# Outputs and last gates of a hybrid encoder layer, made in pairs of pieces

## The chip, the cores and the metric

The kernel runs on one core of one Trainium2 chip. The metric is the device time of one execution in microseconds (us); every time given for the kernel before is the median of three runs, 1471.24 us (1471.11 to 1471.32). Traces are taken from one profiled execution of the same program. The engines are called PE (TensorE, matmuls), PEld (TensorE's weight loads), DVE (VectorE), ACT (ScalarE), POOL (GpSimd) and SP (SyncE); SP, POOL and ACT also issue DMAs.

## The reference, cut to what matters

One encoder layer for T = 1088 frames (1024 of a new stream, 64 of a running one), model width 1024, in fp32. All parts but the norms are matrix products:

```python
proj = xn @ w_in                                   # 1024 -> 5120
cb, cc, ch, q, k, v, ga, gb = split(proj)
cv, conv_state = causal_conv(cc * ch, conv_prefix, w_conv)
ya = (cb * cv) @ w_conv_out                        # 512 -> 1024, "u" is cb * cv
o, new_k, new_v = attn_fn(heads(q), heads(k), heads(v))   # 8 heads of 64
yb = o.reshape(B, L, ATT_DIM) @ w_attn_out         # 512 -> 1024
merged = sigmoid(ga) * ya + sigmoid(gb) * yb
x = x + merged @ w_out                             # 1024 -> 1024
x = x + (silu(xn2 @ w1) * (xn2 @ w3)) @ w2         # d_ff = 2816
```

The change concerns the gates `ga` and `gb`, the two output products `ya` and `yb`, and the start of the products with `w1` and `w3` (the "up" units).

## The kernel before, in words

**Numbers as pairs.** Every fp32 operand is held as a high part, rounded to the fast format by ACT, and a low part, the rest, formed by DVE (`split`, lines 128 and 129). A product is then three matmuls: weight high with x high, weight high with x low, weight low with x high.

**Stages, in order of time.** Norm and transposition of x, and the projection of v; projections for q, k, cc, ch, cb and six of the eight row blocks of gb as seven-product (Strassen-like) units (`run`, line 269); gates ga (eight blocks of 128 rows) and the last two blocks of gb as plain products (`gate`, `product`, lines 333 to 335), with the attention threaded between them; outputs ya and yb with the merge (lines 1097 to 1124); the product with `w_out` (`wo`, lines 1163 to 1168) with the second norm; the up units a0, b0, a1, b1, ... (`run` again); the down products (line 1682).

**Pieces.** T = 1088 columns are four pieces of 272 (`PIECES`; HN = 272, HT = 544). `product` makes one piece: for each block k of 128 rows the three matmuls, all into one PSUM bank. A gate has 8 blocks k, so 24 matmuls a piece; an output block (`ya`, `yb`) has 4, so 12 matmuls a piece. `run` on the other hand works on two pieces, j = 0 and 1, in two banks of one tile [128, 2, 512], and goes (high, high) j = 0, j = 1, then (high, low) j = 0, j = 1, then (low, high) j = 0, j = 1: each weight stands for two matmuls in a row.

**Gates and attention.** The first four gates begin with their pieces 0 and 1, since the right half of x is being loaded again. Then come their pieces 2 and 3 and gates 4 to 7, piece by piece; after each piece `between` emits 3.15 steps of the attention (scores, softmax, transposition, values; 72 of them and three to drain). The last two gates (LAST = 2) stand behind the attention. Gate pieces use three banks (`pmm`); the attention uses five (`patt`, two buffers of two banks, and `ppv`, one). ACT copies a piece to SBUF (line 815, `st_pool`, five buffers) and POOL's queue stores it to DRAM.

**Order of instructions.** The tile framework orders the instructions of every engine at build time: in the program's order, except that an instruction which its own estimate of times finds not ready yet is passed by later ones that are. Engines then run their queue strictly in that order. `tc.issue_after(x)` keeps the instructions of a block behind `x` where they are on the same engine as `x`. A new pool on the place of a closed one waits for the closed pool's tiles.

**Outputs.** When the attention is done, `u` and `ob` (the attention's output) are loaded and split into two tiles; then for two row blocks at a time come ya, ya, yb, yb. Each piece has a bank of `psum2` (five buffers). On a ya piece DVE multiplies by the sigmoid (line 1108); on a yb piece DVE multiplies (1119), adds (1120), and the sum is split into `mg`, the operand of the later products, and, for the 64 frames of the running stream, into `ms`. `gates_in` loads the rows of ga and gb again, ga in four DMAs of a piece each.

**Up units.** Unit a0 (`r0`) and unit b0 (`r1`) are emitted by hand around the last transpositions. The seven steps of a unit are the products 1, 2, 6, 7, 5, 4, 3. a0's and b0's steps 1 and 2 come first, then a0's 6, 7, 5, 4, 3 (behind b0's step 2), then b0's 6 (its third step), 7, 5, 4, 3. `shot` copies (line 257, ACT) keep a product that a later step adds to in the same bank: the snapshot "7" must be taken before step 4 writes.

Of the kernel before, what the change touches and what calls it, by code (L numbers as in the profile page):

```python
# [20 lines left out]
T = TP + TS  # L21
# [11 lines left out]
HT = T // 2  # L33
HN = HT // 2
# [3 lines left out]
LAST = 2  # L38
# [17 lines left out]
class Acts:  # L56
# [3 lines left out]
        self.t = t  # L60

    def at(self, l, k, o, n):
        return self.t[:, l, k, o : o + n]


@with_exitstack
def encoder_kernel(ctx: ExitStack, tc: tile.TileContext, ins, outs):
    nc = tc.nc
    mm = nc.tensor.matmul
    vec, act, pool_e = nc.vector, nc.scalar, nc.gpsimd  # L70
# [24 lines left out]
    u_d = dr.tile([4, P, T], F32, name="u_d")  # L95
# [30 lines left out]
    def split(hi, lo, src):  # L126

        a = act.copy(hi, src)  # L128
        b = vec.tensor_tensor(lo, src, hi.bitcast(F32), op=ALU.subtract)  # L129
        return a.ins, b.ins  # L130
# [11 lines left out]
    taken = [-1]  # L142
# [183 lines left out]
    def product(out, w, x, o, n):  # L326

        kt = 4 * len(w)
        for k in range(kt):
            a, b = (t[:, k % 4] for t in w[k // 4])  # L330
            p, q = x.at(0, k, o, n), x.at(1, k, o, n)
            first, then = (q, p) if x is xn and o // HN % 2 == 0 else (p, q)
            mm(out, a, first, start=k == 0, stop=False)  # L333
            mm(out, a, then, start=False, stop=False)  # L334
            mm(out, b, p, start=False, stop=k == kt - 1)  # L335
# [471 lines left out]
    def gate(i, cs):  # L807
        g, m = GATES[i]
        dst = ga_d if g == "a" else gb_d
        for c in cs:  # L810
            o, n = PIECES[c]
            ps = pmm.tile([P, 512], F32, tag="mm", name=f"g{i}_{c}")
            product(ps[:, :n], gate_w[i], xn, o, n)
            st = st_pool.tile([P, HN], F32, tag="st", name=f"gst{i}_{c}")
            act.copy(st[:, :n], ps[:, :n])
            nc.gpsimd.dma_start(dst[m * P : (m + 1) * P, o : o + n], st[:, :n])

    gate_w = {}
# [216 lines left out]
    sg = {}  # L1035

    def gates_in(nm, m):
        t = row_tile(int(nm == "ga"), f"{nm}{m}")
        if nm == "gb":
            nc.sync.dma_start(t, gb_d[m * P : (m + 1) * P])  # L1040
        for o, n in PIECES:
            sg[nm, m, o] = t[:, o : o + n]
            if nm == "ga":
                nc.sync.dma_start(t[:, o : o + n], ga_d[m * P : (m + 1) * P, o : o + n])

    head_load(0)

# [11 lines left out]
    for i in range(4, len(GATES)):  # L1059
        gate_w[i] = next_w()  # L1060
        if i == len(GATES) - LAST:
            for _ in steps:
                pass
            att_stack.close()
            uo = pg_stack.enter_context(tc.tile_pool(name="uo", bufs=1, reuse_waits="tile"))
            both_x = []
            for nm, pad in (("u", 56), ("ob", 48)):
                uo.tile([P, pad], F32, name=f"pad_{nm}")
                t = uo.tile([P, 2, 4 * T + 8], F32R, name=nm)[:, :, : 4 * T]
                both_x.append(Acts(t.rearrange("p l (k t) -> p l k t", k=4)))  # L1070
            u, ob = both_x
            for q in range(4):
                u_ld = nc.sync.dma_start(u.t[:, 1, q].bitcast(F32), u_d[q])
                u_cast = split(u.t[:, 0, q], u.t[:, 1, q], u.t[:, 1, q].bitcast(F32))[0]
            for k in range(2):
                split(ob.t[:, 0, k], ob.t[:, 1, k], o_rows[k])
            late_r = row_tile(1, "rc2"), row_tile(0, "rc3")
            gates_in("ga", 0)
            gates_in("gb", 0)
            for k, r in zip((2, 3), late_r):  # L1080
                o = ob.t[:, 0, k].bitcast(F32)
                with tc.issue_after(u_ld.ins):
                    nc.sync.dma_start(o, o_d[k * P : (k + 1) * P])
                    ld = rc_load(r, k)
                vec.tensor_tensor(r, o, r, op=ALU.mult)
                split(ob.t[:, 0, k], ob.t[:, 1, k], r)
            with tc.issue_after(ld):
                gates_in("ga", 1)
        for c in range(4):
            gate(i, (c,))  # L1090
            between()


    mg = quarters("mg")
    ms = mspool.tile([P, KD, 2, TS], F32R, tag="ms", name="ms")
    psum2 = pg_stack.enter_context(tc.tile_pool(name="psum2", bufs=5, space=PSUM, reuse_waits="tile"))
    for m0 in range(0, 8, 2):
        for m in (m0, m0 + 1):
            wa = next_w()
            if m0:  # L1100
                gates_in("ga", m)
            for o, n in PIECES:
# [5 lines left out]
                vec.tensor_tensor(t, ya[:, :n], t, op=ALU.mult)  # L1108
        for m in (m0, m0 + 1):
            wb = next_w()  # L1110
            if m:
                gates_in("gb", m)
            for o, n in PIECES:
# [3 lines left out]
                yb = psum2.tile([P, 512], F32, tag="mm", name=f"yb{m}_{o}")  # L1117
                product(yb[:, :n], wb, ob, o, n)
                vec.tensor_tensor(z, yb[:, :n], z, op=ALU.mult)
                vec.tensor_tensor(t, t, z, op=ALU.add)  # L1120
                split(mg.at(0, m, o, n), mg.at(1, m, o, n), t)
                h, a = o // HT, 512 - o % HT
                if a < n:
                    split(ms[:, m, 0, 32 * h : 32 * h + 32], ms[:, m, 1, 32 * h : 32 * h + 32], t[:, a:])
    pg_stack.close()


# [62 lines left out]
    if True:  # L1190
# [578 lines left out]
```

## Time and profile before

| what | value |
|---|---|
| median of three runs | 1471.24 us |
| the profiled execution | 1472.42 us, of which the span of the trace is 1470.3 us |
| matmuls, and weight loads | 10176 each |
| gates, first two pieces of gates 0 to 3 | 344.4 to 368.4 us |
| attention and gate pieces | to 552.1 us |
| rest of the last two gates | 552.1 to 572.9 us |
| outputs ya and yb | 572.9 to 668.9 us |
| product with w_out, second norm | 668.9 to 770.7 us |
| up units | 770.7 to about 1230 us |

A row of a timeline has the start in us from the span's start, the duration, the engine, the source line, the operation, the output and the inputs by the program's names, the shapes, and in brackets how long the engine was idle before and what released it. A row by windows has the stretch, its length, and for each engine the busy time and, in brackets, the count of instructions that touch the stretch. A row by tile has the count, the shortest, median and longest duration in ns, and the first and last start. Matmul durations overlap: what counts for PE is the distance between starts.

### The profile page before, as it was taken

What the parts mean: (1) busy time and instruction counts of PE and PEld (TensorE: products, weight loads), DVE (VectorE), ACT (ScalarE), POOL (GpSimd) and SP (SyncE); (2) the same over time, 40 slices, a digit from 0 to 9 for tenths busy, and PEclk for the clock granted to TensorE, in tenths of its full rate; (3) what the DMA queues carried; (4) which work ended last, traced back from release to release, by engine and by line L of the source; (5) the groups of instructions that cost most, each with busy time, mean ns of one, the idle gap of its engine ahead of it and who ended that gap; (6) DMA issues with size and microseconds to landing.
All of it is one profiled execution on the core that took longest, in us unless ns stands there. A gap on an engine that the chain in (4) does not pass through costs nothing.

```text
span 1470.3 us, 26411 instructions
## 1 busy us (share of the span) xinstructions
PE 1455.5 (99%) x10176; PEld 1366.9 (93%) x10176; DVE 983.1 (67%) x1856; ACT 679.7 (46%) x1391; POOL 136.5 (9%) x249
## 2 busy tenths in 40 slices
PE   8999999999999999999999999999999999999997
PEld 6899999999989899998889999999999999888886
DVE  7975565641677775753588767666666768957677
ACT  7654333332777776531355444444444445512223
POOL 1400010001111111000100111110011111000000
PEclk9999999999999999999999999999999999999999
DMA  8687522237776657434432443443344448867686
GB/s 280 185 274 227 182 78 94 66 111 228 209 192 180 182 172 244 158 126 136 154 108 80 153 168 139 168 150 123 122 153 168 147 168 305 286 228 245 219 265 208
DMA packets 163133, 260.26 MB, mean 177 GB/s; under 512 B 18784, under 2 KB 98848, under 8 KB 163008
## 3 DMA queue, kind: packets, MB, share of 16 engines
q1 hardware_dynamic: 142080, 192.79, 41.6%
q0 software_dynamic: 19776, 63.70, 12.1%
q10 hardware_dynamic: 1152, 2.10, 0.4%
q8 instruction: 80, 1.31, 0.4%
q14 instruction: 45, 0.37, 0.1%
HBM read 170.67 MB, written 89.70 MB: 177 GB/s over the span
## 4 chain that ended last, share of the span: by engine, by line
PE 92%; DVE 3%; DMA 3%; ACT 1%; issue 1%; SPq 1%; ACTq 0%; DVEq 0%
PE Ab L269 9%; PE Aa L269 8%; PE A L1682 8%; PE Db L269 4%; PE Da L269 4%; PE D L1682 4%; PE Agb L269 2%; PE Bb L269 2%; PE Ba L269 2%; PE B L1682 2%; PE wo L1163 2%; PE wo L1165 2%; PE wo L1164 2%; PE g L335 2%; PE g L334 2%; PE g L333 2%
## 5 line engine op out<-in xcount | busy, mean ns | idle before, releaser
L333 PE MATMUL g<-xn,wp 128*128 128x272 f32 x320 | 93.7, 293 | 0.0
L335 PE MATMUL g<-xn,low 128*128 128x272 f32 x320 | 93.4, 292 | 0.0
L334 PE MATMUL g<-xn,wp 128*128 128x272 f32 x320 | 92.7, 290 | 0.0
L128 ACT CAST ring<-w2r 128x512 fp32r<-128x512 f32 (+1 forms) x78 | 43.2, 588 | 98.4 <-PE A L1682 50.7
L865 DVE CUSTOM_DVE_ANT_0 p<-s,bb 128x640 f32<-128x640 f32 (+5 forms) x72 | 47.5, 660 | 38.5 <-DMA qd<-q_d 26.2
L1682 PE MATMUL A<-ring,low 128*128 128x512 f32 x264 | 72.3, 389 | 0.0
L1682 PE MATMUL A<-ring,ht 128*128 128x512 f32 x264 | 72.3, 390 | 0.0
L129 DVE TENSOR_TENSOR low<-rawa,wa 128x512 fp32r<-128x512 f32 x55 | 37.7, 687 | 41.7 <-ACT wa L128 41.7
L335 PEld LDWEIGHTS g<-xn,low 128*128 128x128 f32 x320 | 60.3, 188 | 0.5
L333 PEld LDWEIGHTS g<-xn,wp 128*128 128x128 f32 x320 | 60.3, 188 | 0.5
L334 PEld LDWEIGHTS g<-xn,wp 128*128 128x128 f32 x320 | 60.2, 188 | 0.5
L1682 PEld LDWEIGHTS A<-ring,ht 128*128 128x128 f32 x264 | 49.4, 188 | 10.6 <-ACT acc L1692 0.4
L1682 PEld LDWEIGHTS A<-ring,low 128*128 128x128 f32 x264 | 49.6, 188 | 10.3
L269 PE MATMUL Ab<-tt,wb 128*128 128x272 f32 x352 | 57.8, 285 | 1.3 <-ACT wb L128 1.3
L129 DVE TENSOR_TENSOR ring<-w2r,ring 128x512 fp32r<-128x512 f32 (+1 forms) x78 | 49.0, 646 | 13.4 <-ACT ring L128 13.2
L269 PE MATMUL Ab<-mg,wb 128*128 128x272 f32 x352 | 58.0, 285 | 0.0
L269 PE MATMUL Aa<-tt,wa 128*128 128x272 f32 x352 | 57.8, 285 | 0.0
L269 PE MATMUL Aa<-mg,wa 128*128 128x272 f32 x352 | 57.7, 285 | 0.0
L875 ACT ACTIVATE p<-p,mx 128x640 f32<-128x640 f32 (+5 forms) x72 | 50.8, 706 | 11.4 <-DVE mx L865 10.1
L128 ACT CAST wa<-rawa 128x512 fp32r<-128x512 f32 x55 | 34.0, 621 | 47.4 <-PE Ab L269 33.3
L128 ACT CAST wb<-rawb 128x512 fp32r<-128x512 f32 x55 | 34.0, 620 | 38.7 <-PE Aa L269 24.5
L1163 PE MATMUL wo<-low,mg 128*128 128x512 f32 x128 | 50.9, 397 | 0.0
(554 smaller groups left out, 4547.9 us busy)
## 6 DMA issues: line engine op xcount, KB each, us to landing
h_d<-hq POOLq DMA_DIRECT2D x44, 512.0 KB, 4.4
ht<-h_d SPq DMA_DIRECT2D x77, 256.0 KB, 3.9
low<-h_d SPq DMA_DIRECT2D x77, 256.0 KB, 3.7
h_d<-hq_early POOLq DMA_DIRECT2D x29, 512.0 KB, 4.6
rawa<-in_w_ff SPq DMA_DIRECT2D x11, 1024.0 KB, 6.2
rawb<-in_w_ff SPq DMA_DIRECT2D x11, 1024.0 KB, 5.5
w2r<-in_w_ff SPq DMA_DIRECT2D x11, 1024.0 KB, 7.9
qd<-q_d SPq DMA_DIRECT2D x32, 272.0 KB, 4.1
```

Source lines behind the costliest of these rows:

```text
L128: a = act.copy(hi, src)
L129: b = vec.tensor_tensor(lo, src, hi.bitcast(F32), op=ALU.subtract)
L269: newest[0] = mm(t[:, j, :HN], w[:, k, :], x[p][:, k, l, j * HN : (j + 1) * HN], start=p in (1, 2, 7) and k == 0 and n == 0, stop=k == 3 a ...
L333: mm(out, a, first, start=k == 0, stop=False)
L334: mm(out, a, then, start=False, stop=False)
L335: mm(out, b, p, start=False, stop=k == kt - 1)
L865: vec.tensor_tensor_reduce(out=s if len(ps.shape) == 2 else s.rearrange("p (a b) -> p a b", a=2), in0=ps, in1=bias if len(ps.shape) == 2 e ...
L875: act.activation(s, s, AF.Exp, bias=mx, scale=-1.0, accum_out=sm)
L1163: mm(ps, x(k, 0), wh, start=f, stop=False)
L1164: mm(ps, x(k, 1), wh, start=False, stop=False)
L1165: mm(ps, x(k, 0), wl, start=False, stop=e)
L1682: mm(t, ht[k][:, j, x], w[:, l], start=p in (1, 2, 7) and k == 0 and n == 0, stop=k == len(ks) - 1 and n == 2, skip_group_check=p in (6, 5 ...
```

## The change

Gate pieces that are emitted two at a time are now made in the order of `run` by the new `product2`: the first pieces of gates 0 to 3, in two of the three `pmm` banks, and both halves of the last two gates, in a two-bank tile. The outputs are made in halves of 544 columns, also with `product2`; DVE and ACT work on a half at once, and ga's rows come in two DMAs instead of four. `psum2` is opened when the attention's pools close, with two buffers of two banks instead of five of one; the last two gates use it too. `st_pool` has three buffers instead of five. `u` and `ob` get a layout in which each half of 544 has 32 more words behind it and the low parts lie 40 words further; the low parts of their weights start at the slot's beginning instead of 40 words on, and the skipped slot before `w_out` is no longer skipped. In the up stage, b0's third step is put behind the last matmul of a0.

```diff
 class Acts:
     def at(self, l, k, o, n):
-        return self.t[:, l, k, o : o + n]
+        h = o // HT
+        a = h * (HT + 32) + o - h * HT
+        return self.t[:, l, k, a : a + n]
...
+    def product2(outs, w, x, o):
+
+        kt = 4 * len(w)
+        for k in range(kt):
+            a, b = (t[:, k % 4] for t in w[k // 4])
+            for n, (s, l) in enumerate(((a, 0), (a, 1), (b, 0))):
+                for j in range(2):
+                    mm(
+                        outs[j], s, x.at(l, k, o + j * HN, HN),
+                        start=k == 0 and n == 0, stop=k == kt - 1 and n == 2,
+                    )
...
-            {"src": ins[nm][0][:, m * P : (m + 2) * P], "w": 2 * P, "at": 40}
+            {"src": ins[nm][0][:, m * P : (m + 2) * P], "w": 2 * P}
...
-    st_pool = pg_stack.enter_context(tc.tile_pool(name="st_pool", bufs=5, reuse_waits="tile"))
+    st_pool = pg_stack.enter_context(tc.tile_pool(name="st_pool", bufs=3, reuse_waits="tile"))
...
     def gate(i, cs):
         g, m = GATES[i]
         dst = ga_d if g == "a" else gb_d
-        for c in cs:
+        if i >= len(GATES) - LAST:
+            two = psum2.tile([P, 2, 512], F32, tag="mm", name=f"g{i}_{cs[0]}")
+            pss = [two[:, j] for j in range(2)]
+        else:
+            pss = [pmm.tile([P, 512], F32, tag="mm", name=f"g{i}_{c}") for c in cs]
+        if len(cs) == 2:
+            product2([ps[:, :HN] for ps in pss], gate_w[i], xn, PIECES[cs[0]][0])
+        else:
+            product(pss[0][:, :HN], gate_w[i], xn, *PIECES[cs[0]])
+        for c, ps in zip(cs, pss):
             o, n = PIECES[c]
-            ps = pmm.tile([P, 512], F32, tag="mm", name=f"g{i}_{c}")
-            product(ps[:, :n], gate_w[i], xn, o, n)
             st = st_pool.tile([P, HN], F32, tag="st", name=f"gst{i}_{c}")
             act.copy(st[:, :n], ps[:, :n])
...
             att_stack.close()
+            psum2 = pg_stack.enter_context(tc.tile_pool(name="psum2", bufs=2, space=PSUM, reuse_waits="tile"))
...
-        for c in range(4):
-            gate(i, (c,))
-            between()
+        if i < len(GATES) - LAST:
+            for c in range(4):
+                gate(i, (c,))
+                between()
+        else:
+            gate(i, (0, 1))
+            gate(i, (2, 3))
...
-    psum2 = pg_stack.enter_context(tc.tile_pool(name="psum2", bufs=5, space=PSUM, reuse_waits="tile"))
...
-            for o, n in PIECES:
+            for o in HALVES:
                 t = sg["ga", m, o]
                 with tc.issue_after(u_cast):
                     act.activation(t, t, AF.Sigmoid)
-                ya = psum2.tile([P, 512], F32, tag="mm", name=f"ya{m}_{o}")
-                product(ya[:, :n], wa, u, o, n)
-                vec.tensor_tensor(t, ya[:, :n], t, op=ALU.mult)
+                ya = psum2.tile([P, 2, 512], F32, tag="mm", name=f"ya{m}_{o}")
+                product2([ya[:, j, :HN] for j in range(2)], wa, u, o)
+                t = t.rearrange("p (j n) -> p j n", j=2)
+                vec.tensor_tensor(t, ya[:, :, :HN], t, op=ALU.mult)
...
         two_sums = early.tile([P, 2, D], F32, tag="raw", name="two_sums")
-        taken[0] += 1
         w = wo_half(0)
...
             r = up_run(n, this, ahead)
+        if n == 1:
+            with tc.issue_after(newest[0]):
+                next(r)
         for _ in r:
```

The loop of yb is changed in the same way, with the add and both splits on halves.

More of the change, by code (lines that the diff above doesn't have):

```diff
@@ L62, in at, with rows @@
     def at(self, l, k, o, n):
-        return self.t[:, l, k, o : o + n]
+        h = o // HT
+        a = h * (HT + 32) + o - h * HT
+        return self.t[:, l, k, a : a + n]
+    def rows(self, l, k):
+        return self.t[:, l, k].rearrange("p (h t) -> p h t", h=2)[:, :, :HT]
 @with_exitstack
@@ L1035, in encoder_kernel @@
     sg = {}
+    HALVES = (0, HT)
     def gates_in(nm, m):
@@ L1064, in encoder_kernel @@
             att_stack.close()
+            psum2 = pg_stack.enter_context(tc.tile_pool(name="psum2", bufs=2, space=PSUM, reuse_waits="tile"))
             uo = pg_stack.enter_context(tc.tile_pool(name="uo", bufs=1, reuse_waits="tile"))
             both_x = []
[L1067 removed]
+            for nm, pad in (("u", 24), ("ob", 24)):
                 uo.tile([P, pad], F32, name=f"pad_{nm}")
[L1069 to L1070 removed]
+                t = uo.tile([P, 8 * 2 * (HT + 32) + 40], F32R, name=nm)
+                n = 8 * (HT + 32)
+                t = bass.AP(tensor=t.tensor, offset=t.offset, ap=[t.ap[0], [n + 40, 2], [2 * (HT + 32), 4], [1, 2 * (HT + 32)]])
+                both_x.append(Acts(t))
             u, ob = both_x
             for q in range(4):
[L1073 to L1074 removed]
+                u_ld = nc.sync.dma_start(u.rows(1, q).bitcast(F32), u_d[q].rearrange("p (h t) -> p h t", h=2))
+                u_cast = split(u.rows(0, q), u.rows(1, q), u.rows(1, q).bitcast(F32))[0]
             for k in range(2):
[L1076 removed]
+                split(ob.rows(0, k), ob.rows(1, k), o_rows[k].rearrange("p (h t) -> p h t", h=2))
             late_r = row_tile(1, "rc2"), row_tile(0, "rc3")
@@ L1101, in encoder_kernel @@
                 gates_in("ga", m)
-            for o, n in PIECES:
+            for o in HALVES:
                 t = sg["ga", m, o]
@@ L1112, in encoder_kernel @@
                 gates_in("gb", m)
-            for o, n in PIECES:
+            for o in HALVES:
                 t, z = sg.pop(("ga", m, o)), sg.pop(("gb", m, o))
@@ L1116, in encoder_kernel @@
                     act.activation(z, z, AF.Sigmoid)
-                yb = psum2.tile([P, 512], F32, tag="mm", name=f"yb{m}_{o}")
-                product(yb[:, :n], wb, ob, o, n)
-                vec.tensor_tensor(z, yb[:, :n], z, op=ALU.mult)
+                yb = psum2.tile([P, 2, 512], F32, tag="mm", name=f"yb{m}_{o}")
+                product2([yb[:, j, :HN] for j in range(2)], wb, ob, o)
+                z2 = z.rearrange("p (j n) -> p j n", j=2)
+                vec.tensor_tensor(z2, yb[:, :, :HN], z2, op=ALU.mult)
                 vec.tensor_tensor(t, t, z, op=ALU.add)
[L1121 to L1124, printed above, removed]
+                split(mg.at(0, m, o, HT), mg.at(1, m, o, HT), t)
+                h = o // HT
+                split(ms[:, m, 0, 32 * h : 32 * h + 32], ms[:, m, 1, 32 * h : 32 * h + 32], t[:, 512:])
     pg_stack.close()
```

11 lines of the change are left out of this document (6 added, 5 removed).

## The prediction

> **What bounds the kernel now.** I read the page first: who is busy, and what the chain that ended last consists of.
>
> ```profile
> span 1470.3 us, 26411 instructions
> ...
> PE 1455.5 (99%) x10176; PEld 1366.9 (93%) x10176; DVE 983.1 (67%) x1856; ACT 679.7 (46%) x1391; POOL 136.5 (9%) x249
> ...
> PE 92%; DVE 3%; DMA 3%; ACT 1%; issue 1%; SPq 1%; ACTq 0%; DVEq 0%
> ...
> L269 PE MATMUL Ab<-tt,wb 128*128 128x272 f32 x352 | 57.8, 285 | 1.3 <-ACT wb L128 1.3
> ```
>
> PE sets the end, so only two things count: the distance between matmul starts, and holes in PE's queue. The last row is the one hole outside the attention that the page names: 1.3 us before unit b's step 6. Next the view by windows, on stretches that hold one kind of matmul (272 columns each):
>
> ```profile
> core 0: us, PE busy (x) PEld busy (x) DVE busy (x) ACT busy (x) POOL busy (x), PEclk, DMA share, GB/s
> 344.38:368.38 24.00, 24.00 (x195) 24.00 (x194) 0.69 (x1) 3.85 (x9) 3.82 (x7) 1.00 0.89 270
> 552.08:572.90 20.82, 20.82 (x168) 20.82 (x168) 12.58 (x14) 14.60 (x25) 3.57 (x7) 1.00 0.87 290
> 572.90:668.92 96.02, 96.02 (x771) 96.02 (x769) 63.71 (x157) 43.30 (x120) 0.54 (x1) 1.00 0.44 139
> 822.00:1130.00 308.00, 308.00 (x2500) 308.00 (x2499) 205.62 (x345) 138.10 (x259) 39.51 (x75) 1.00 0.43 151
> ```
>
> PE is never idle in any of them and its clock is whole. The counts hold two or three matmuls that straddle the edges. In the order of `product`: 24.00 us / 192 = 125.0 ns in the first gates and 96.02 / 768 = 125.0 ns in the outputs. In the order of `run` (fourth row): 308.00 / 2498 = 123.3 ns.
>
> **Pair order: -2.0 us.** It covers 768 matmuls of the outputs, 192 of the last two gates and 192 of the first four gates' left halves: 1152 x 1.7 ns = 1.96 us. Which part of the 1.7 ns is order and which is where the operands lie is not shown. Bounds: at the worst the new places cost as much as the order gives, +2.0; at the best twice the difference, -3.9. I take the difference itself, since `u` and `ob` get the same distances between halves and parts as `run`'s operands have (1152 words a block, 272 a piece, 40 beyond a multiple of 64 between the parts).
>
> [...]
>
> **The attention's tail: +1.6 us.** The last two gates move from `pmm` to banks that the attention frees. The timeline of PE at its end:
>
> ```profile
> 545.34 0.29 PE L335 MATMUL g<-xn,low 128*128 128x272 f32 x1
> 545.46 0.71 PE L954 MATMUL t<-ident,p 128*128 128x128 f32 x5
> 545.93 0.37 PE L333 MATMUL g<-xn,wp 128*128 128x272 f32 x1
> ...
> 546.66 0.22 PE L929 MATMUL t<-ident,p 64*64 64x64 f32 x1
> ...
> 548.28 0.28 PE L334 MATMUL g<-xn,wp 128*128 128x272 f32 x1
> 548.40 0.27 PE L937 MATMUL rt<-ident,sm 128*9 128x128 f32 x1
> 548.42 1.41 PE L979 MATMUL pv<-pt,vd 128*128 128x512 f32 x6
> 549.67 0.29 PE L335 MATMUL g<-xn,low 128*128 128x272 f32 x1
> ...
> 551.23 0.92 PE L966 MATMUL pv<-pts,vsd 128*128 128x128 f32 x5
> ```
>
> After 552.08 there are 166 gate matmuls (168 in the window less two at its edge), so 26 of the last two gates' 192 stand before it: 12 from 549.67 on, 14 between 545.93 and 548.40. They fill waits, which DVE's timeline shows:
>
> ```profile
> 545.29 0.82 DVE L129 TENSOR_TENSOR pt<-t,pt 128x640 fp32r<-128x640 f32 x1 [0.24 <-ACT pt L128]
> ...
> 547.42 0.82 DVE L129 TENSOR_TENSOR pt<-t,pt 128x640 fp32r<-128x640 f32 x1 [0.27 <-ACT pt L128]
> ...
> 549.10 0.22 DVE L129 TENSOR_TENSOR pts<-t,pts 64x64 fp32r<-64x64 f32 x1 [0.52 <-ACT pts L128]
> ```
>
> The values at 548.42 need DVE's `pt`, which ends at 548.24. The last transposed tile leaves its banks at 549.32; a pair of banks is free for the gates from then on, not before. Gate 7's matmuls are used up at 545.93, so PE has only five small transpositions left until 548.3: 14 x 0.125 = 1.75 us of filling are lost, 0.1 of it won back as the values start without a queue. The 12 later ones can stay. Bounds: 0 if the build-time order keeps other gate work for the hole; +3.1 if it puts all 26 behind.
>
> **b0's third step: +0.4 us.** The timelines of PE, ACT and DVE around the page's hole:
>
> ```profile
> 793.39 0.41 PE L269 MATMUL Aa<-tt,low 128*128 128x272 f32 x2
> 795.10 0.76 PE L269 MATMUL Ab<-tt,wb 128*128 128x272 f32 x4 [1.30 <-ACT wb L128]
> 795.70 0.68 PE L269 MATMUL Da<-mg,wa 128*128 128x272 f32 x4
> ```
>
> ```profile
> 793.27 0.66 ACT L1331 ACTIVATE sa<-sa 128x544 f32<-128x544 f32 x1
> 794.43 0.62 ACT L128 CAST wb<-sf 128x512 fp32r<-128x512 f32 x1 [0.50 <-DVE sf L221]
> 794.95 0.61 ACT L257 COPY sa<-Da 128x544 f32<-128x544 f32 x1
> ```
>
> Four matmuls of b0's step 6 stand ahead of a0's step 4 (`Da<-mg`) and wait for a cast, which waits for DVE. With the change step 4 is next in PE's queue. But it writes the bank whose snapshot ACT takes at 794.95, behind that same cast, to 795.56. So PE would wait from 793.64 to 795.61 rather than to 795.10; step 4 starts 0.09 us earlier than now and the four matmuls (0.49 us) come later: +0.4. The edit adds its order on PE alone, so nothing moves the snapshot. Queued behind the waiting matmul are a0's steps 4 and 3 and all of b0; nobody else waits for them sooner than now. Bounds: +0.4, and -1.5 if ACT's queue comes out with the snapshot ahead of the cast.
>
> **Evictions and buffers.** Rows by tile, and where the outputs end:
>
> ```profile
> L1108 DVE TENSOR_TENSOR ga<-ya,ga x32: 429/442/444, 574.6 to 657.1; 128x272 f32<-128x272 f32 x32
> L1329 DVE TENSOR_TENSOR sa<-Aa,sa x11: 714/718/725, 796.1 to 1204.0; 128x544 f32<-128x544 f32 x11
> L815 ACT COPY gst<-g x40: 366/387/392, 347.6 to 573.1; 128x272 f32<-128x272 f32 x40
> DMA to landing us min/median/max: 2.0/3.7/7.9
> ```
>
> Halves are cheaper than pieces for DVE: 0.72 us against 2 x 0.44. But a pair of banks must be evicted before the half after next: 24 x 0.123 - 0.17 = 2.8 us after its last matmul ends. The longest lag that I find now is at the first change from ya to yb:
>
> ```profile
> 584.79 0.29 PE L335 MATMUL ya<-u,low 128*128 128x272 f32 x1
> ...
> 586.10 0.69 DVE L129 TENSOR_TENSOR low<-rawp,wp 128x512 fp32r<-128x512 f32 x1 [2.03 <-ACT wp L128]
> 586.71 0.43 DVE L1108 TENSOR_TENSOR ga<-ya,ga 128x272 f32<-128x272 f32 x1
> ...
> 589.06 0.44 DVE L129 TENSOR_TENSOR mg<-ga,mg 128x272 fp32r<-128x272 f32 x1 [0.49 <-ACT mg L128]
> ```
>
> From 585.08 to 587.14 are 2.06 us, with the longer multiplication 2.35: it holds, with 0.45 to spare; 0. In the first gates two of three banks are taken by each pair, so the second bank of the next is free only after an ACT copy (0.39): three places of 0.4 us, which the build can fill with the other bank's matmuls: +0.2 (bounds 0 and 1.2). Three instead of five `gst` buffers: a pair comes each 5.9 us and a store lands in 3.7, at most 7.9; ACT may be held for 2 us, PE not, as its next pair has banks: 0 (bound 0.5). ACT's Sigmoids and ga's fewer DMAs lie beside 3 us a half of PE: 0. The last half's multiplication, add, cast and two subtractions must be done when `w_out`'s product, from sample frames on, comes to its last block:
>
> ```profile
> 668.92 0.40 PE L1167 MATMUL wo<-low,ms 128*128 128x512 f32 x1
> ...
> 671.13 0.18 DVE L129 TENSOR_TENSOR ms<-ga,ms 128x32 fp32r<-128x32 f32 x1
> ```
>
> `ms` is done at 671.31; its block 7 is due 14 x 0.23 us after 668.92, at 672.1. The chain grows by 0.3 for each of three DVE operations: 0.1 late, +0.1 (bounds 0 and 0.8).
>
> **Sum.** -2.0 + 1.6 + 0.4 + 0.2 + 0.1 = +0.3. The profiled execution took 1472.42 us (span 1470.3, 2.1 around it), 1.2 above the median; both shift alike, so the forecast is 1471.24 + 0.3 = 1471.5 us.
>
> **Rivals.**
>
> *Both holes shut (faster).* The build keeps work for the tail, and the snapshot comes ahead of the cast: -2.0 - 1.5 + 0.1 = -3.4, 1467.8 us. For it: the queues' order is made from estimates, and all stages before change; ACT was idle for 0.50 us ahead of the cast, in which the snapshot would fit. Against: nothing in the edits reaches either. Chance 0.26. Only one of the two: -1.6 or -1.3, about 1469.8, chance 0.13.
>
> *The pair buffers bind (slower).* In yb DVE has per half 0.72 + 0.72 + 0.72 + 0.18 and half of a 0.69 weight split: 2.7 us of 2.96. If it waits in its queue for ACT's cast between add and subtraction, as at 589.06 above (0.49 idle), and for the weights' cast, each half takes 3.7: 0.7 over, four halves a stretch, four stretches, 11.2 us; the 2 us of slack each stretch begins with are taken off, 3.2 remain: 1474.7, and 1476.7 where ya starts late too. It decides once DVE's half passes 2.96 us. For it: 90% load and two buffers for five. Against: DVE does other work in most such waits today. Chance 0.23.
>
> *The order is not what helps.* The 1.7 ns come from addresses, or are given back by them: +2.3, 1473.5 us, chance 0.08.
>
> *One load for two matmuls.* Matmuls of 512 and 272 columns stand 0.227 (6.80 us for 30) and 0.125 us apart, so 9 ns of each are not columns; 576 loads saved would be -5.2 more, 1466.3 us, chance 0.02 (the counts of loads speak against it).
>
> ```profile
> 1274.82 6.80 PE A L1682 x30
> ```
>
> [...]
>
> **Chances.** Forecast 0.28. Faster by over 0.2% (2.9 us; about what a measurement of this kernel can tell from no change): 0.26 + 0.02 = 0.28. Within: 0.28 + 0.13 + 0.08 = 0.49. Slower: 0.23. Range: down to 1467.0 to take in the two shut holes, up to 1476.5 for the pair buffers; left out are one load for two and the far ends. The forecast's own case reaches from 1470 to 1473.
>
> **What would show it.** Pair order: 123.3 ns in windows on the outputs; 125 refutes it. Tail: PE idle for about 1.6 us before the values near 548; no such row refutes it. Third step: PE waiting for ACT's copy `sa<-Da` rather than for `wb`; a0's step 4 starting right behind step 5 refutes it. Buffers: idle PE before `ya` or `yb` on DVE's rows. The forecast is wrong if two of these turn the same way.

## The result, and the profile after

| | median us | runs | lowest to highest |
|---|---|---|---|
| before | 1471.24 | 9 | 1470.77 to 1473.20 |
| after | 1475.03 | 9 | 1473.19 to 1477.22 |

The ratio is 1.0023 [1.0015, 1.0032]: slower, by a little over the 0.2% that the prediction took as what a measurement can tell from no change. The forecast was 1471.5 us; the range, up to 1476.5, holds the time. The profiled execution of after is its fastest (1473.19 us, span 1471.1), so the trace has to explain two things: what is longer in it, and why most executions are 1 to 4 us longer still.

The head of the page of after: PE's share is as before, and DVE has 64 instructions fewer.

```profile
span 1471.1 us, 26282 instructions
...
PE 1454.0 (99%) x10176; PEld 1364.9 (93%) x10176; DVE 977.2 (66%) x1792; ACT 674.0 (46%) x1343; POOL 136.5 (9%) x249
...
PE 90%; DVE 4%; DMA 2%; ACT 2%; issue 1%; SPq 1%; ACTq 0%
```

The view by windows of after, on the first gates, the outputs, and the wait ahead of the first unit's step 4 (length, then the busy time and count of PE, PEld, DVE, ACT and POOL):

```profile
343.47:368.00 24.53, 24.51 (x195) 23.90 (x193) 0.69 (x1) 3.35 (x8) 3.27 (x6) 1.00 0.89 261
574.47:669.28 94.81, 94.81 (x771) 94.80 (x769) 57.97 (x95) 38.95 (x77) 1.08 (x2) 1.00 0.41 138
794.89:796.11 1.22, 0.29 (x4) 0.08 (x2) 1.22 (x3) 1.19 (x3) 0.00 (x0) 1.00 0.32 68
```

The outputs are 1.21 us shorter than before (96.02): 94.81 / 768 = 123.4 ns. The first gates are 0.58 us longer (before, 23.95 us pass from their first start to the start behind them; the window shown of before ends 0.05 later), though their matmuls are in the new order. The third row is mostly waiting.

PE at the attention's end, in the timeline of after, and DVE beside it:

```profile
546.00 0.46 PE L950 MATMUL t<-ident,p 64*128 64x64 f32 x4
546.30 0.22 PE L953 MATMUL t<-ident,p 64*64 64x64 f32 x1
548.46 0.28 PE L961 MATMUL rt<-ident,sm 128*9 128x128 f32 x1 [1.95 <-DVE pt L134]
548.50 1.42 PE L1003 MATMUL pv<-pt,vd 128*128 128x512 f32 x6
549.75 0.66 PE L349 MATMUL g<-xn,wp 128*128 128x272 f32 x4
```

```profile
546.65 0.69 DVE L134 TENSOR_TENSOR low<-rawp,wp 128x512 fp32r<-128x512 f32 x1
547.26 0.41 DVE L907 TENSOR_TENSOR co<-ca 64x256 f32<-64x256 f32 x1
547.60 0.81 DVE L134 TENSOR_TENSOR pt<-t,pt 128x640 fp32r<-128x640 f32 x1
```

The idle stretch stands where it was forecast. It is 1.95 us long, because a weight split (`low`) now stands ahead of `co` and `pt`; before, DVE made two of these in a row earlier:

```profile
543.64 1.28 DVE L129 TENSOR_TENSOR low<-rawp,wp 128x512 fp32r<-128x512 f32 x2
```

So `pt` starts 1.08 us after the end of PE's last transposition (546.52), where it started 0.54 us after it before (547.42 and 546.88).

The start of `w_out`'s product, PE and DVE:

```profile
672.28 0.40 PE L1202 MATMUL wo<-wo,ms 128*128 128x512 f32 x1
673.05 0.50 PE L1201 MATMUL wo<-low,ms 128*128 128x512 f32 x1 [0.37 <-DVE ms L134]
```

```profile
670.74 0.72 DVE L1155 TENSOR_TENSOR ga<-ga,gb 128x544 f32<-128x544 f32 x1
672.17 0.72 DVE L134 TENSOR_TENSOR mg<-ga,mg 128x544 fp32r<-128x544 f32 x1 [0.71 <-ACT mg L133]
672.81 0.18 DVE L134 TENSOR_TENSOR ms<-ga,ms 128x32 fp32r<-128x32 f32 x1
```

From one start to the next are 0.77 us instead of 0.23: block 7 waits 0.54 us for `ms`, which stands behind `mg`, a cast and a subtraction of 544 columns. In the kernel before a weight split (670.18) stood between the addition and this subtraction, in the time of the cast; now it stands ahead of the addition (670.13), and DVE waits 0.71 us for the cast.

And b0's third step, PE and ACT:

```profile
794.77 0.41 PE L274 MATMUL Aa<-tt,low 128*128 128x272 f32 x2
796.11 0.77 PE L274 MATMUL Da<-mg,wa 128*128 128x272 f32 x4 [0.93 <-ACT sa L262]
```

```profile
794.92 0.62 ACT L133 CAST wb<-sf 128x512 fp32r<-128x512 f32 x1 [0.50 <-DVE sf L226]
795.45 0.61 ACT L262 COPY sa<-Da 128x544 f32<-128x544 f32 x1
```

Step 4 waits for the snapshot, and the snapshot stands behind the cast, as forecast.

Stage by stage, from the starts of the same matmuls in both traces (us that a stage is longer than before; the second column is the changed kernel profiled once more, in an execution of 1475.57 us; the start of `w_out` reaches to the first transposition `xt`, and the next row goes on from there):

| stage | after | once more |
|---|---|---|
| first gates | +0.58 | +0.58 |
| attention and last gates | +1.90 | +3.26 |
| outputs | -1.21 | 0.00 |
| start of `w_out` | +0.63 | +0.63 |
| from there to the end of b0 | 0.00 | +0.01 |
| rest | -0.25 | -0.10 |
| sum | +1.65 | +4.38 |

The sums start at the first gate. Up to there both kernels run the same work; the profiled execution of before comes there at 344.38 us, the others at 342.9 to 344.4. So the trace of after explains some 1.7 us. The other execution is 2.7 us longer, 1.36 of it in the attention's stage and 1.21 in the outputs; the remaining executions have no trace.

### The profile page after: what moved, and what is told of

Read it like the earlier page. It is cut to its first block, busy times and chain, and to the rows that moved or that the text cites. A ratio compares the mean times of both kernels' runs of the same rounds, so it can differ in the third digit from the quotient of the medians.

```text
span 1471.1 us, 26282 instructions
## 1 busy us (share of the span) xinstructions
PE 1454.0 (99%) x10176; PEld 1364.9 (93%) x10176; DVE 977.2 (66%) x1792; ACT 674.0 (46%) x1343; POOL 136.5 (9%) x249
## 3 DMA queue, kind: packets, MB, share of 16 engines
q8 instruction: 80, 1.31, 0.4%
## 4 chain that ended last, share of the span: by engine, by line
PE 90%; DVE 4%; DMA 2%; ACT 2%; issue 1%; SPq 1%; ACTq 0%
PE Ab L274 9%; PE Aa L274 8%; PE A L1718 8%; PE Db L274 4%; PE Da L274 4%; PE D L1718 4%; PE ya L349 3%; PE yb L349 3%; PE Agb L274 2%; PE B L1718 2%; PE Bb L274 2%; PE Ba L274 2%; PE wo L1197 2%; PE wo L1199 2%; PE wo L1198 2%; PE t L978 2%
## 5 line engine op out<-in xcount | busy, mean ns | idle before, releaser
L338 PE MATMUL g<-xn,wp 128*128 128x272 f32 x192 | 57.0, 297 | 0.0
L340 PE MATMUL g<-xn,low 128*128 128x272 f32 x192 | 56.4, 294 | 0.0
L339 PE MATMUL g<-xn,wp 128*128 128x272 f32 x192 | 55.8, 291 | 0.0
L1197 PE MATMUL wo<-low,mg 128*128 128x512 f32 x128 | 50.9, 397 | 0.0
L1199 PE MATMUL wo<-wo,mg 128*128 128x512 f32 x128 | 50.1, 391 | 0.0
L1198 PE MATMUL wo<-low,mg 128*128 128x512 f32 x128 | 50.0, 390 | 0.0
L134 DVE TENSOR_TENSOR pt<-t,pt 128x640 fp32r<-128x640 f32 (+2 forms) x64 | 41.7, 651 | 12.1 <-ACT pt L133 11.3
```

Source lines behind the costliest of these rows:

```text
L1197: mm(ps, x(k, 0), wh, start=f, stop=False)
L1198: mm(ps, x(k, 1), wh, start=False, stop=False)
L1199: mm(ps, x(k, 0), wl, start=False, stop=e)
```

## The experiments

Two theories at the start: the idle stretch at the attention's end costs more than its length, because of the clock; or it costs its length, and the spread comes from elsewhere. The kernel before ran beside each of the three groups that follow, with a median of 1471.68, 1471.50 and 1471.40 us.

### The idle stretch: there or not, filled, and put into the kernel before

The changed kernel once more:

> The changed kernel once more, unaltered, as the yardstick for the other three on the same chip. Its median so far was 1475.03 us, with runs from 1473.2 to 1477.2; the profiled execution explains only 0.8 us of the 3.8 that it is above the kernel before. Theory 1 (the idle stretch of PE at the attention's end costs more in most executions than its own 2.1 us, because it lowers the granted clock for a while after it) and theory 2 (the stretch costs its own 1.7 us and the spread has another source) both expect some 1475 us here with a spread of 3 to 4 us.

The last two gates in pieces, as before (their banks come from `pmm` again, which is not shown):

```diff
...
-            gate(i, (0, 1))
-            gate(i, (2, 3))
+            for c in range(4):
+                gate(i, (c,))
+                between()
```

> The changed kernel with the last two gates computed piece by piece in pmm's banks, as before the change; everything else as changed. 14 of their matmuls can stand in the attention's last wait again. Theory 1: no long idle stretch, so the spread goes with it: 1470.5 to 1471.5 us, runs within 1 us. Theory 2: 1.6 us of idle PE are won back and 0.3 us of pair order in the last gates lost: 1473.7 us, spread as in the changed kernel.

The stretch filled (the products of `fill` are not read by anything):

```diff
             for _ in steps:
                 pass
+            fill = pmm.tile([P, 512], F32, tag="mm", name="fill")
+            for n in range(14):
+                mm(fill[:, :HN], gate_w[i][n % 2][0][:, n % 4], xn.at(0, n % 4, 0, HN), start=True, stop=True)
             att_stack.close()
```

> The changed kernel with 14 extra matmuls of 272 columns whose sums nobody reads, put into PE's queue ahead of the last two gates so that the idle stretch is filled (14 x 0.125 = 1.75 us of work that is not the reference's). Theory 1: the time no longer pays for what idleness does to the clock, only for the stretch itself: about 1473 us, runs within 1 us. Theory 2: filling saves nothing: 1475 us, spread as in the changed kernel.

The kernel before, with gate 8's first piece behind the transposition `rt`:

```diff
...
+            if i == len(GATES) - LAST and c == 0:
+                with tc.issue_after(last_rt[0]):
+                    gate(i, (c,))
...
```

> The kernel before with one edit: the first piece of gate 8 has to stand behind the transposition of row sums at the attention's end, so that PE gets the same idle stretch of some 1.7 to 2 us there. Theory 1: 1474 to 1475 us with a spread of 3 to 4 us, as in the changed kernel. Theory 2: the stretch costs itself: 1472.9 us, runs as close together as those of the kernel before.

| | median us | runs | lowest to highest | ratio to before |
|---|---|---|---|---|
| a0_again | 1476.21 | 6 | 1474.84 to 1483.97 | 1.0040 [1.0025, 1.0056] |
| e1_last_pieces | 1471.64 | 11 | 1470.75 to 1478.99 | 1.0004 [0.9996, 1.0013] |
| e2_filled | 1473.67 | 11 | 1473.22 to 1475.12 | 1.0016 [1.0007, 1.0025] |
| e3_before_hole | 1474.36 | 11 | 1472.51 to 1475.27 | 1.0016 [1.0007, 1.0024] |

Theory 1 holds. Without the stretch (e1_last_pieces) the median is that of the kernel before, but for one run of 1478.99 us. Fourteen matmuls more make the changed kernel 2.5 us faster, though they last 1.75 us, and about as much (2.0) is what e2_filled stays above e1_last_pieces. The kernel before becomes 2.7 us slower by one idle stretch of 1.6 us, and its runs fall into two groups: four from 1472.5 to 1473.3 with a mean clock of 0.999, seven from 1474.4 to 1475.3 with 0.997 or 0.998 (0.998 occurs in the kernel before too, 0.997 does not). The traces show the clock itself. The changed kernel once more, by windows (PEclk is the column behind POOL):

```profile
540.00:548.22 8.22, 6.26 (x50) 5.56 (x48) 7.34 (x16) 5.85 (x13) 0.55 (x1) 1.00 0.51 162
548.22:551.63 3.41, 3.41 (x13) 3.03 (x14) 0.77 (x3) 0.94 (x3) 2.02 (x4) 0.50 0.64 176
551.63:575.55 23.92, 23.92 (x194) 23.78 (x194) 11.31 (x13) 13.29 (x21) 2.74 (x5) 1.00 0.79 235
```

The same view of e3_before_hole, and one row of PE's timeline of each of the two:

```profile
547.49:550.90 3.41, 3.41 (x14) 3.11 (x13) 1.02 (x3) 0.92 (x3) 2.02 (x4) 0.50 0.13 27
```

```profile
548.17 2.44 PE L1003 MATMUL pv<-pt,vd 128*128 128x512 f32 x6
```

```profile
547.15 0.28 PE L937 MATMUL rt<-ident,sm 128*9 128x128 f32 x1 [1.61 <-DVE pt L129]
```

Right behind the idle stretch the granted clock is halved for 3.41 us, and the six products that took 1.42 us in the trace of after take 2.44; the gate matmuls behind them are slowed as well: in e3_before_hole they start 0.23 us apart from 549.20 to 550.79, and 0.12 from 550.98 on. That is the 1.36 us by which the attention's stage is longer in the second column of the table. In e1_last_pieces 16 gate matmuls stand in the wait, and in e2_filled the fill; the 16 start 0.12 or 0.13 us apart from the second on (546.71 to 548.46), and the granted clock of e2_filled is 1.00. PE of e1_last_pieces from the first to the last of the 16, and the window of e2_filled in which PE is busy for 5.96 of 6.00 us:

```profile
546.33 0.22 PE L949 MATMUL t<-ident,p 64*64 64x64 f32 x1
546.47 0.40 PE L340 MATMUL g<-xn,low 128*128 128x272 f32 x1
...
548.46 0.29 PE L340 MATMUL g<-xn,low 128*128 128x272 f32 x1
548.58 0.27 PE L957 MATMUL rt<-ident,sm 128*9 128x128 f32 x1
```

```profile
546.00:552.00 6.00, 5.96 (x44) 5.21 (x43) 3.92 (x8) 3.85 (x11) 1.41 (x3) 1.00 0.56 182
```

Why not in every execution? In the two traces with a drop, the clock records have full speed for 539.31 us before it, 3.41 us of the drop, and full speed for 918.18 us after it; in before and after they have full speed from 7.38 and 7.56 us on, for 1457.49 and 1460.90 us, up to a halved clock behind the last matmul. These lengths are 158, 1, 269, 427 and 428 times 3.413 us. So in these four traces the clock changes only at ticks 3.413 us apart, which do not begin with the wait. Counted on from the first record, the ticks at 544.81 and 548.22 of a0_again have all of its 1.95 us between them; in the trace of after, whose clock stayed whole, a tick at 546.87, by the same count, cuts the stretch into 0.4 and 1.6 us. But the length of the idleness between two ticks is not all that counts: in e5_no_third (below) PE idles for 1.68 us between two ticks, more than the 1.61 of e3_before_hole, and its clock stays whole. The times from tick to tick of a0_again, e3_before_hole, after and e5_no_third, in this order:

```profile
544.81:548.22 3.41, 1.45 (x15) 1.06 (x13) 3.29 (x6) 2.33 (x5) 0.55 (x1) 1.00 0.32 122
544.08:547.49 3.41, 1.79 (x16) 1.36 (x15) 2.99 (x5) 2.41 (x7) 0.55 (x1) 1.00 0.92 273
546.87:550.28 3.41, 1.82 (x12) 1.64 (x13) 2.09 (x5) 1.31 (x5) 1.04 (x3) 1.00 0.58 168
601.29:604.70 3.41, 1.73 (x15) 1.51 (x14) 2.85 (x6) 2.80 (x7) 0.00 (x0) 1.00 0.31 92
```

A halved clock followed the first two, a whole one the last two. PE's busy time alone does not part them (1.79 against 1.73), but in these four the kind of work does: without the transpositions (inputs `ident`), PE is busy for 0.36 and 0.69 us in the first two, for 1.79 and 1.73 in the last two. Near the ends of the programs, where PE runs out of work, a halved clock followed 1.27 us of products in before (1461.46 to 1464.87) and a whole one 1.81 us in after (1461.64 to 1465.05). That transpositions count for less than products is an estimate from these six times; no run varied the length of the stretch or the work around it.

### Buffers of the gates' copies, and the third step

Five `gst` buffers, for which `u` and `ob` lie closer:

```diff
-        a = h * (HT + 32) + o - h * HT
+        a = h * (HT + 8) + o - h * HT
...
-    st_pool = pg_stack.enter_context(tc.tile_pool(name="st_pool", bufs=3, reuse_waits="tile"))
+    st_pool = pg_stack.enter_context(tc.tile_pool(name="st_pool", bufs=5, reuse_waits="tile"))
```

> The changed kernel with five buffers for the gates' copies instead of three; the room comes from u and ob, whose halves lie 552 words apart instead of 576 (1104 a block instead of 1152). Theory A: three buffers hold ScalarE for 2 to 3 us behind the stores of gb_d, and that delays ob and then the outputs' first multiplications, which cost PE 1.2 us in one of two profiled executions. Then no gst copy waits over 1 us for a DMA, no product of the outputs waits, and the median is some 0.5 us lower, 1474.5 to 1475 us. Theory B: the wait comes from the late multiplications themselves, whatever the stores do: PE waits for `ga` as before, 1475 to 1476 us. If the distance of 576 is what makes the pair order pay, the outputs' pitch goes back to 125 ns and the time up by 1.3 us; if not it stays at 123.3. The idle stretch at the attention's end stays.

The third step's place taken back, on top of e1_last_pieces:

```diff
...
-        if n == 1:
-            with tc.issue_after(newest[0]):
-                next(r)
```

> The changed kernel with the last two gates in pieces (as in e1_last_pieces) and without the third step's new place. Theory A, the prediction's: four matmuls of b0's step 6 go back into the wait for the snapshot, so 0.4 us are saved against e1_last_pieces: 1471.2 us, and PE waits for ACT's wb for 1.3 us and not for its copy sa. Theory B: step 4 of the first unit is due just as late either way and the four matmuls only change places: 1471.6 us, as e1_last_pieces.

`ms` first, the first gates in single pieces, and five buffers with the layout of e4_five_stores (not shown again), on top of e1_last_pieces; then the same without the third step's place:

```diff
-        gate(i, (0, 1))
+        gate(i, (0,))
+        gate(i, (1,))
...
-                split(mg.at(0, m, o, HT), mg.at(1, m, o, HT), t)
                 h = o // HT
                 split(ms[:, m, 0, 32 * h : 32 * h + 32], ms[:, m, 1, 32 * h : 32 * h + 32], t[:, 512:])
+                split(mg.at(0, m, o, HT), mg.at(1, m, o, HT), t)
```

> e1_last_pieces with three more edits: the first four gates' left halves in single pieces, as before the change; the split of ms ahead of that of mg; five gst buffers with halves 552 words apart. If the three places were sized rightly in the trace of the changed kernel, 0.6 us are saved in the first gates, 0.5 at the start of w_out's product and 0.0 to 0.4 in the outputs against e1_last_pieces: 1470.3 to 1470.6 us. If waits only move on: 1471 to 1471.6.

> e6_all_third without the third step's new place: what is left of the change are the outputs by pairs and halves, with ms first. If each saving adds, 0.4 us less than e6_all_third, 1470.0 us, which is 1.2 to 1.7 us below the kernel before. If step 4's place decides nothing: as e6_all_third.

| | median us | runs | lowest to highest | ratio to before |
|---|---|---|---|---|
| e4_five_stores | 1476.40 | 6 | 1475.11 to 1482.35 | 1.0040 [1.0026, 1.0053] |
| e5_no_third | 1471.61 | 11 | 1470.36 to 1472.95 | 1.0000 [0.9991, 1.0008] |
| e6_all_third | 1472.49 | 12 | 1471.34 to 1482.29 | 1.0015 [1.0002, 1.0028] |
| e7_all | 1471.72 | 11 | 1470.65 to 1473.64 | 1.0003 [0.9994, 1.0011] |

The medians of e4, e6 and e7 lie above what was expected, and that of e5 is where theory B had it, while its trace speaks for A. The traces say why.

*Buffers.* With three buffers ACT is held by stores. a0_again, ACT, DVE and PE:

```profile
574.97 0.39 ACT L839 COPY gst<-g 128x272 f32<-128x272 f32 x1 [3.09 <-DMA gb_d<-gst]
```

```profile
580.66 1.29 DVE L134 TENSOR_TENSOR ob<-rc,ob 128x1088 fp32r<-128x1088 f32 x1 [0.57 <-ACT ob L133]
581.87 1.35 DVE L1142 TENSOR_TENSOR ga<-ya,ga 128x544 f32<-128x544 f32 x2
```

```profile
582.64 0.52 PE L349 MATMUL ya<-u,wp 128*128 128x272 f32 x2 [1.02 <-DVE ga L1142]
```

The copy waits 3.09 us for a store, the cast of `ob` behind it on ACT is late, then DVE's split of `ob`, the first multiplications behind that, and PE, which has only two pairs of banks. In the trace of after the longest such wait is 1.95 us and PE passes; from 545 to 657 us ACT's instructions stand in the same order in both traces. In e4_five_stores no gst copy waits for a DMA there, and no product of the outputs waits. So theory A holds for the wait, as far as one execution shows. But a load can do the same. e5_no_third has no such store wait:

```profile
600.02 1.28 ACT L1130 ACTIVATE ga<-ga 128x544 f32<-128x544 f32 x2 [2.29 <-DMA ga<-ga_d]
```

```profile
601.85 0.69 DVE L134 TENSOR_TENSOR low<-rawp,wp 128x512 fp32r<-128x512 f32 x1 [3.08 <-ACT wp L133]
```

```profile
603.97 0.77 PE L349 MATMUL ya<-u,wp 128*128 128x272 f32 x4 [1.68 <-DVE ga L1134]
```

Here a Sigmoid at the head of ACT's queue waits 2.29 us for its row of `ga`; the weight cast behind it is late, DVE's split of `low` behind that, and the multiplication that frees a pair of banks. The spread of e5_no_third's runs, from 1470.4 to 1472.9, would fit such a wait in some of them, but only this one execution has a trace.

*Distance.* e4, e6 and e7 lose what they save in the outputs: with 552 words from half to half these take 96.4 us, more than the 96.0 before. That was the disputed part of the gain, and the next runs are about it.

*Third step.* From the end of the first unit's step 5 to the end of b0, e1_last_pieces is 0.48 us longer than e5_no_third, and e6_all_third 0.48 us longer than e7_all. PE in e5_no_third, to compare with the row at 796.11 above:

```profile
795.53 0.77 PE L274 MATMUL Ab<-tt,wb 128*128 128x272 f32 x4 [0.41 <-ACT wb L133]
796.14 0.67 PE L274 MATMUL Da<-mg,wa 128*128 128x272 f32 x4
```

Four matmuls stand in the wait again, and step 4 starts 4.14 us after the start of step 5, where it is 4.05 in after. The medians of e1 and e5 do not show it (1471.64, 1471.61); the wait of 1.68 us above, in the outputs of e5's profiled execution, may hide it. Those of e6 and e7 are 0.77 apart, with a wide spread in e6.

*`ms` and first gates.* In e6 and e7 `w_out`'s product starts without a wait (0.65 us less than in after), and the first gates take 23.95 us, as before.

### Order or places

The outputs with all else put right, in four versions. f2_spaced is e7_all with the change's own layout and three buffers:

> e7_all with the change's own layout again (halves of u and ob 576 words apart, three gst buffers): of the change, only the outputs by pairs and halves are left, with ms first. Theory A: the places of the halves set the pitch of the outputs, which is 123.3 ns here and 125.4 in e7_all; that is 1.5 us, so 1470.1 us, up to 1.8 more in the executions in which PE waits for the first multiplication of a ya stretch. Theory B: the pitch falls one way or the other by chance in each kernel: 1471.7 us as e7_all.

The old order of matmuls in that layout:

```diff
...
-                product2([ya[:, j, :HN] for j in range(2)], wa, u, o)
+                for j in range(2):
+                    product(ya[:, j, :HN], wa, u, o + j * HN, HN)
```

(and the same for `yb`)

> f2_spaced with the outputs' matmuls in the old order, one piece of 272 columns after the other, while the layout, the pairs of banks and the halves stay. Theory A1, the prediction's: the order by pairs brings the 1.7 ns, so the pitch goes back to 125.0 and the time to 1.3 us above f2_spaced, 1471.4 us. Theory A2: the places alone bring them: 123.3 ns and the time of f2_spaced.

The pair order in the layout of before (`HT + 0`, 8 words between the parts, five `gst` buffers), and with 560 words (four buffers):

> f2_spaced with u and ob laid out as in the kernel before (halves 544 words apart, 1088 a block, 8 between the parts; five gst buffers), the order by pairs kept. Theory A1: the order brings the gain: 123.3 ns, the time of f2_spaced or a little less, as PE waits less often. Theory A2: the places bring it: 125 ns or more, 1471.4 us or more.

> f2_spaced with halves 560 words apart, 1120 a block, and four gst buffers, for which that makes room. If a distance of 576 is needed, 125 ns or more and 1471.4 us; if 560 will do, 123.3 ns and 1470.1 us or less.

f1 to f4 were measured beside 33 runs of before; e7_all is from the group ahead (before 1471.50), so only its ratio compares.

| | halves apart | order | outputs, ns | median us | runs | ratio to before |
|---|---|---|---|---|---|---|
| before | 544 | piece | 125.0 | 1471.40 | 33 | |
| f3_old_layout | 544 | pairs | 125.1 | 1470.93 | 11 | 0.9993 [0.9985, 1.0002] |
| e7_all | 552 | pairs | 125.5 | 1471.72 | 11 | 1.0003 [0.9994, 1.0011] |
| f4_560 | 560 | pairs | 125.4 | 1471.28 | 11 | 0.9995 [0.9987, 1.0004] |
| f1_piece_order | 576 | piece | 124.7 | 1471.14 | 11 | 0.9995 [0.9986, 1.0004] |
| f2_spaced | 576 | pairs | 123.3, from 625.5 us on 125.4 | 1470.39 | 11 | 0.9989 [0.9981, 0.9998] |

The pitch comes from windows inside the outputs (less two matmuls at the edges). f1_piece_order, f3_old_layout, f4_560, e7_all:

```profile
572.00:667.40 95.40, 95.40 (x767) 95.40 (x766) 57.97 (x94) 38.70 (x78) 0.89 (x2) 1.00 0.43 141
```

```profile
573.00:668.70 95.70, 95.70 (x767) 95.70 (x767) 58.04 (x95) 38.87 (x76) 0.54 (x1) 1.00 0.42 138
```

```profile
571.90:667.80 95.90, 95.90 (x767) 95.90 (x766) 57.92 (x95) 38.70 (x76) 0.54 (x1) 1.00 0.42 137
```

```profile
571.80:667.80 96.00, 96.00 (x767) 96.00 (x767) 58.19 (x95) 38.90 (x76) 0.54 (x1) 1.00 0.42 139
```

In these traces neither theory holds alone. The order without the places gives nothing (125.1), the places without the order 0.3 ns, both together 1.7 while the faster rhythm lasts. One trace of each would be little, but the others agree: with pairs and 576 words the outputs begin at 123.3 ns in all six traces (after, a0_again, e1, e2, e5, f2), with pairs and another distance in none of five (e4, e6, e7, f3, f4). The last two gates agree too. Their operand `xn`, which `run` also reads, lies in the same places in both kernels; their matmuls stand 125.4 ns apart before (20.82 / 166), in pairs in after 20.35 / 165 = 123.3:

```profile
554.00:574.35 20.35, 20.35 (x168) 20.35 (x167) 10.45 (x10) 14.41 (x21) 3.30 (x6) 1.00 0.88 276
```

f2_spaced is 1.0 us faster than the kernel before, by the interval 0.02 to 0.19%, and the best of all versions here. It has two buffers of pairs and three of `gst` as the changed kernel has, so its outputs can still wait.

Its profiled execution does not keep the faster rhythm. Two windows of its outputs, which come to 124.4 ns as a whole:

```profile
572.00:625.00 53.00, 53.00 (x432) 53.00 (x431) 33.96 (x54) 23.68 (x47) 0.54 (x1) 1.00 0.51 168
629.00:667.50 38.50, 38.50 (x309) 38.50 (x308) 23.47 (x40) 13.83 (x28) 0.00 (x0) 1.00 0.25 80
```

53.00 / 430 = 123.3 ns, then 38.50 / 307 = 125.4: same operands, same order, clock whole.

## Why the prediction came out as it did

The forecast was +0.3 us, the median is 3.8 above the kernel before. By the prediction's own border of 2.9 us that is "slower", which had a chance of 0.23, but the rival that stood for it, pair buffers that bind in yb, is not what happened. The range holds the time because its upper end was set for that rival; that the time stays inside is in part luck, since the halved clock, 1.36 us where a trace shows it, stands nowhere in the prediction.

*Pair order, -2.0.* For the outputs the size is right where PE does not wait: 1.31 was the share of their 768 matmuls, 1.21 came in after. The reason was left open in the prediction, and by the traces neither half of it is the cause alone. For the first gates the step failed: 0.33 was to be saved and the three borders between pairs to cost 0.2; they cost 0.9 (24.53 us against 23.95 in e7_all's single pieces and in before, with the 0.33 that the order should have saved), within the bound of 1.2 given.

*The attention's tail, +1.6.* **This is the term that was furthest off where the clock was halved.** Place and mechanism were right: PE idle for 1.95 us, waiting for `pt`, because the last gates wait for the attention's banks. The size was not: the step priced an idle stretch at its own length. With the 0.33 of its pair order the stage was to be 1.3 us longer; it was 1.9 where the clock stayed whole and 3.3 where it was halved behind the stretch. e1 to e3 show that the stretch does it. Of the first 0.6, 0.54 is `pt` starting later behind a weight split. In the execution with the halved clock, 4.4 us above before, 2.0 of the 4.1 us that the forecast misses are here; 1.3 are in the outputs, 0.7 in the first gates and 0.5 at `ms`, less 0.4 at b0's third step.

*b0's third step, +0.4.* Right: 0.48 us, by the wait that was forecast. In after the sum of that stage is nevertheless zero, as the queues of the stage stand in another order: counted from the first `Aa`, the cast `wb` that the snapshot stands behind starts 23.23 us on, and 23.73 before (794.92 - 771.69; 794.43 - 770.70). PE comes to the wait 0.4 us later, since transpositions `xt` stand earlier in its queue and wait for DVE's `xg`, but that is taken up by the wait. Nothing in the prediction named this. The row of after:

```profile
772.94 0.77 PE L1269 MATMUL xt<-ident,xg 128*128 128x128 f32 x5 [0.58 <-DVE xg L1258]
```

*Evictions and buffers, 0.* Right in the trace of after, wrong in others: 1.0 us in a0_again, 1.7 in e5_no_third. The slack was worked out at the change from ya to yb, and the rival "the pair buffers bind" for DVE's load in yb; what uses it up is one wait for a DMA at the head of ACT's queue, early in a ya stretch, behind which casts stand that DVE needs. The prediction had let ACT be held for 2 us by a store and PE not. Without store waits, e4 had no wait of the first kind.

*`ms`, +0.1.* It was 0.63. The prediction lengthened the chain by DVE's three operations only. ACT's cast of `mg` between them grew too (0.42 to 0.65 us), and the weight split that lay in its time before now stands ahead of the addition, so that DVE waits 0.71 us (at 672.17).

*Rivals.* Both holes are open, as forecast. The sum of the first rival, -3.4, leaves out the 0.2 of the first gates; by the prediction's own terms it is -3.2. No run shows the saved loads from which the last rival's 5.2 us are worked out: after has 10176 loads for 10176 matmuls, as before.

## What to carry to other kernels

Here the stage with an idle stretch of PE of 1.95 us came out 1.90 us longer in one profiled execution and 3.26 in another, where the granted clock was 0.50 for 3.41 us behind it; one of 1.61 us put 2.7 us on the median of the kernel before. So such a stretch is worth filling, with products that nobody reads if nothing else is ready (fourteen of them took 2.5 us off the median of the changed kernel); by the estimate from these traces, one between transpositions sooner than one between products. A change that takes work out of a wait has to be priced with what the wait does to the clock, and with more than one profiled execution. Where fewer and larger buffers replace many small ones, follow each queue for the longest wait for a DMA at its head (3.09 us on ACT in a0_again, 2.29 in e5_no_third), not only the load of the engine that empties the buffers.

## What the hardware showed that was not expected

*Two rhythms at one clock.* In the order of `run`, the same matmuls of 272 columns stand 123.3 or 125.5 ns apart. The up stage of after and of e4_five_stores (whose profiled execution took 1482.35 us):

```profile
850.00:1000.00 150.00, 150.00 (x1219) 150.00 (x1218) 105.01 (x177) 67.79 (x129) 20.75 (x39) 1.00 0.44 154
```

```profile
850.00:1000.00 150.00, 150.00 (x1197) 150.00 (x1196) 101.47 (x172) 66.90 (x127) 20.89 (x40) 1.00 0.45 157
```

150 / 1217 = 123.3 and 150 / 1195 = 125.5 ns, both with PEclk 1.00. In e4 the slower rhythm begins with the first matmul after the wait for the snapshot (797.44 us) and lasts to the end of the up stage, some 3400 matmuls, for which e4 takes 7.8 us longer than a0_again. In f2_spaced it begins within the outputs at 625.5 us, behind two distances of 140 and 201 ns. In the traces of after, a0_again, e1, e2 and e5 the ten matmuls or so behind a short wait stand 125 ns apart too, and the next are back at 123.3. Single executions of a0_again, e1 and e6 that took 1479 to 1484 us would fit the loss that e4 shows; only e4's has a trace. What decides whether the faster rhythm comes back stays open, and with it why 552, 560 and 544 words stayed in the slower one in the executions profiled here. The place of the weights' low parts, which the change moves too, was not varied.
